# A hybrid decoder step on one core: 1088 token columns in three chunks instead of four

## The chip, the cores and the metric

The kernel runs on one core of one Trainium2 chip, as one program. The time is the device time of one execution in microseconds (us), the median of several runs. The core has five engines with instruction streams of their own: TensorE (PE in the profile, its weight loads PEld), VectorE (DVE), ScalarE (ACT), GpSimd (POOL) and SyncE (SP), which here issues most of the transfers.

## The reference, cut to what matters

Two layers work on 1024 prompt tokens and on 8 sampled sequences of 8 tokens, 1088 tokens in all, with 1024 features.

```
for layer in range(2):
    xn = rmsnorm(x, g_mix)
    x += rg_block(xn)   if layer == 0   # gate = gelu(xn Wy); conv4(xn Wx) -> gated linear recurrence -> Wout
    x += gla_block(xn)  if layer == 1   # 4 heads, chunked linear attention with decay, chunk 64
    x += cross_attn(rmsnorm(x, g_xa))   # 4 heads over 256 memory tokens, softmax
    x += W2 @ relu(W1 @ rmsnorm(x, g_mlp))**2      # hidden 4096
y = rmsnorm(x, g_final)
```

Before the layers the prompt's memory keys and values are computed for both layers (`mem_kv`). Everything is float32 to the caller.

## The kernel before, in words

**Layout.** Activations lie with features on the 128 partitions and tokens as columns. The columns are cut into chunks (`COL`, `WID`, lines 20 and 21): four of 256, 256, 256 and 320 columns, the last with the 64 sampled tokens. `TILES` lists the blocks of 128 tokens in each chunk.

**Products.** A float32 product is made of three products of `float32r` parts: each weight and each activation is split into a high part (a copy on ACT) and a low part (a subtraction on DVE), and `mm3` (lines 94 to 98) issues high x high, high x low and low x high into one PSUM bank. A weight tile of 128 x 128 is the stationary operand, a chunk's columns are the moving one. So each of these three passes of each weight tile costs one TensorE instruction per chunk. `gemm_in` (line 236) makes 48 of them per chunk and pair of weight units (2 output tiles, 8 input tiles, 3 passes), `gemm_out` (line 263) also 48 (8 output tiles, 2 input tiles, 3 passes); `gemm_out` puts `512 // w` output tiles into one PSUM bank and adds each bank into the residual with one DVE instruction (line 276). `gemm_tok` (line 251) has tokens as the stationary operand and 256 weight columns moving; it works by tiles of 128 tokens.

**Weights.** They come as units of 512 KB in the order of use, each loaded into a `raw` buffer by SP (`pump`, line 144), split on ACT and DVE (lines 183 and 184) into a ring of five. A phase may have further `raw` buffers (`more_raw`).

**Order.** The phases are `mem_kv`, `rg`, `xattn(0)`, `mlp(0)`, `gla`, `xattn(1)`, `mlp(1)`. In each, an outer loop goes over groups of weights (4 groups in `rg`, 4 heads in `xattn` and `gla`, 16 groups in `mlp`) and an inner one over chunks. `gemm_out` of a chunk isn't issued at once but put into a queue (`queue_out`, `pend`) and taken out by `pop` behind a later product; `tick` does the same for the small matmuls of the norm (`rstd_sum`, `rstd_row`). A framework places the waits and the final order of each engine: an instruction that isn't ready can be passed by later ones of the program, as the trace shows, and a buffer of a tag with `bufs` copies is handed on when its last reader is done.

**rg** (lines 522 to 657), per group and chunk: `X` (product, 4-tap convolution on DVE, split), `G` (small products, sigmoid, the recurrence as a scan), `Y` (product, gelu, times the recurrence's result, split), then the queued `gemm_out`. **xattn** (693): `Q`, `scores` and softmax, transposes, `p_v`; with the last chunk of each head also the sampled sequences, whose 16 blocks of keys and values of 256 KB come through the buffers `kvt`. **mlp** (660): product in, squared relu, split, product out. **gla** (876): `V` and `G` by token tiles, `z_chain` (decay) and `QK` by chunks, `core_a` (transposes and scores), `core_b`: the state `S` goes from 64 tokens to the next 64 in a serial chain of one matmul (line 1023) and one DVE instruction (line 1026); at a head's last chunk four loads of sampled states (`load_s0`) are used, updated and stored.

Of the kernel before, what the change touches and what calls it, by code (L numbers as in the profile page):

```python
# [22 lines left out]
TILES = [[(0, 0, 128), (1, 128, 128)], [(2, 0, 128), (3, 128, 128)], [(4, 0, 128), (5, 128, 128)],  # L23
         [(6, 0, 128), (7, 128, 128), (8, 256, 64)]]
MAXW = max(WID)

# Rows of the table of per-feature vectors.
# [4 lines left out]
# Units of weights that each phase takes.  # L32
# [7 lines left out]
def strided(ap, dims):  # L40
    """The elements of a tile slice's first one onwards, in other free dims."""
    return bass.AP(tensor=ap.tensor, offset=ap.offset, ap=[list(ap.ap[0])] + [list(d) for d in dims])


class Step:
# [145 lines left out]
    def get(self):  # L191
        """The next two units: [(index, hi, lo), ...]."""
# [43 lines left out]
    def gemm_in(self, us, c, banks=None):  # L236
        """Features on partitions: two tiles of 128 outputs for chunk c."""
# [13 lines left out]
    def gemm_tok(self, us, c, t0, tw, out):  # L251
        """Tokens on partitions: 256 outputs for the tokens t0..t0+tw of chunk c."""
# [10 lines left out]
    def gemm_out(self, us, hT, c, norm=None, last=False):  # L263
        """Two tiles of hidden features into the residual of chunk c."""
# [51 lines left out]
    def inv_rms(self, out, ms, rows, cols):  # L316
        """out = 1 / sqrt(ms + EPS), ms in PSUM or SBUF; one Newton step on what the tables give."""
# [11 lines left out]
    def rstd_sum(self, c, norm):  # L329
# [28 lines left out]
    def table(self, ins=None):  # L358
        """Exp and Ln from one table; behind the activation ins."""
# [25 lines left out]
    def mem_kv(self):  # L385
# [6 lines left out]
        # the second layer's parts wait where the last chunk's activations will go  # L392
# [90 lines left out]
    def rg_consts(self):  # L483
# [7 lines left out]
        # log(1 + e) = 2 artanh(e / (2 + e))  # L491
# [14 lines left out]
    def rg_gate_w(self, g):  # L506
        """The gates' 64 x 64 blocks of two feature tiles, as block-diagonal 128 x 128."""
# [14 lines left out]
    def rg(self, next_norm):  # L522
        nc, a = self.nc, self.a
        self.new_phase("rg", 1)
# [4 lines left out]
        def Y(us, us_o, g, c):  # L529
# [4 lines left out]
            z = self.t("gy", [128, 2, MAXW], F32, 2)[:, :, :w]  # L534
# [11 lines left out]
        def X(us, g, c):  # L546
# [5 lines left out]
            w = WID[c]  # L552
            xc[c] = self.t("xc", [128, 2, MAXW], F32, 3)
            todo = []
            for f in range(2):
                ff = 2 * g + f
                s = self.t("xs", [128, 3 + 256 + 88], F32, 2)
# [29 lines left out]
        def G(gw, g, c):  # L587
# [11 lines left out]
            # sqrt(1 - e ** 2) with 1 - e ** 2 = (1 + e ** 2) * tanh(-log(e))  # L599
# [20 lines left out]
            if c < NC - 1:  # L620
                nc.gpsimd.tensor_copy(self.hl_prev[:, 2 * g:2 * g + 2], h[:, :, 255])
# [5 lines left out]
        for g in range(4):  # L627
# [65 lines left out]
    def xattn(self, l, next_norm):  # L693
        nc, a = self.nc, self.a
        norm = V_XA + l
        self.new_phase(f"xa{l}", 1)
        # the sampled queries, each sequence's 8 in a group of 32 columns (the other 24 are zero)
# [21 lines left out]
        def Q(h, c):  # L719
# [14 lines left out]
            qh = self.t("qh", [128, 2, 256], R32)  # L734
            ql = self.t("ql", [128, 2, 256], R32)
# [3 lines left out]
        def softmax(p, out):  # L739
            mx = self.small("mx", 2)  # L740
            sm = self.small("smx", 2)
            pv = p.rearrange("p (t m) -> p t m", t=2)
            nc.vector.tensor_reduce(mx, pv, AX.X, OP.max, negate=True)
            for t in range(2):
                nc.scalar.activation(out[:, t, :], pv[:, t, :], AF.Exp, bias=mx[:, t:t + 1], accum_out=sm[:, t:t + 1])
            nc.vector.reciprocal(sm, sm)
            for t in range(2):
                nc.vector.tensor_scalar(out[:, t, :], out[:, t, :], sm[:, t:t + 1], None, op0=OP.mult)

        def scores(h, c):  # L750
            qh, ql = st["q"]
            kh, kl = st["k"]
            p = self.pm()
            for t in range(2):
                o = p[:, t * 256:t * 256 + 256]
                ts = slice(t * 128, t * 128 + 128)
                for dt in range(2):
                    mm = nc.tensor.matmul
                    mm(o, qh[:, dt, ts], kh[:, dt, :], start=dt == 0, stop=False)
                    mm(o, qh[:, dt, ts], kl[:, dt, :], start=False, stop=False)  # L760
                    mm(o, ql[:, dt, ts], kh[:, dt, :], start=False, stop=dt == 1)
            P = self.t("P", [128, 2, 256])
            softmax(p, P)
            st["P", c] = P

        def p_trans(h, c):
            P = st.pop(("P", c))
            p = self.pm()
            for mt in range(2):
                for t in range(2):  # L770
                    nc.tensor.transpose(p[:, mt * 256 + t * 128:mt * 256 + t * 128 + 128],
                                        P[:, t, mt * 128:mt * 128 + 128], self.ident)
            hh, hl = self.hidden()
            pv = p.rearrange("p (a b) -> p a b", a=2)
            split(hh[:, :, :256], hl[:, :, :256], pv)
            st["PT"] = (hh, hl)

        def p_v(h, c):
            ph_, pl = st.pop("PT")
            vh, vl = st["v"]  # L780
            hT = self.hidden()
            for dt in range(2):
                p = self.pm()
                ds = slice(dt * 128, dt * 128 + 128)
                for mt in range(2):
                    self.mm3(p[:, :256], vh[:, mt, ds], vl[:, mt, ds], ph_[:, mt, :256], pl[:, mt, :256], mt == 0, mt == 1)
                split(hT[0][:, dt, :256], hT[1][:, dt, :256], p[:, :256])
# [15 lines left out]
        def turn(src):  # L803
            """[(i, 32), o, (s, 128)] -> [128, s, o, (i, 32)]"""
# [12 lines left out]
        def sample_p(h):  # L817
            P = self.t("P", [128, 2, 256])
# [3 lines left out]
        def sample_v(h, P, hT):  # L822
# [6 lines left out]
            ot = self.t("q", [128, 2, 256])  # L829
            nc.vector.tensor_copy(ot.rearrange("p a b -> p (a b)"), so)  # L830
# [45 lines left out]
    def gla(self, next_norm):  # L876
# [7 lines left out]
        nc.gpsimd.memset(smask[:, 0:256].rearrange("p (n t) -> p n t", t=64)[:, :, 0], 0.0)  # L884
        nc.gpsimd.memset(smask[:, 256:320].rearrange("p (n t) -> p n t", t=8)[:, :, 0], 0.0)
        # [s, t]: 1 where s <= t within a chunk
# [7 lines left out]
        # block of 8: s // 8 == t // 8, i.e. 0 <= s - 8 * (t // 8) <= 7  # L894
# [3 lines left out]
        tri8 = self.t("tm", [128, MAXW])[:64, :64]  # L898
# [32 lines left out]
        def z_chain(h, c):  # L931
# [10 lines left out]
            m = self.t("tm", [128, MAXW], F32, 1)[:, :w]  # L942
# [6 lines left out]
            nc.vector.tensor_tensor_scan(bc, smask[:, :w], m, 0.0, OP.mult, OP.add)  # L949
# [3 lines left out]
            for t0, n, L, g0 in ((0, 4, 64, 0),) + (((256, 8, 8, 4),) if c == NC - 1 else ()):  # L953
# [32 lines left out]
        def core_a(h, c):  # L986
# [19 lines left out]
        def load_s0(h, b):  # L1006
            s0 = self.t("s0", [128, 2, 256], F32, 3)
# [217 lines left out]
```

## Time and profile before

| | us |
|---|---|
| median of 3 runs | 3169.61 (3167.9 to 3169.88) |
| span of the profiled execution | 3166.8 |
| median minus that span | 2.81 |
| TensorE busy in the profile | 3116.2, 24287 matmuls |
| VectorE, ScalarE, GpSimd busy | 1768.8, 1093.6, 213.9 |
| transfers | 195.54 MB, mean 62 GB/s |

The profile is one execution. It gives no time around its span, so the span is what a sum is made against, and the 2.81 us to the median are added as they are. Matmuls are pipelined: a row's duration is the time from start to modelled end of one, and consecutive ones overlap, so that what a matmul costs in a row of them is the distance between starts.

### The profile page before, as it was taken

The numbers are of one execution on the slowest core, as the hardware profiler recorded it, in microseconds if no ns is written. First come the engines' busy times: TensorE is split into PE (matmuls) and PEld (weight loads), VectorE is DVE, ScalarE is ACT, GpSimd is POOL, SyncE is SP. The second block draws the span as 40 slices with busy tenths as digits, with TensorE's granted clock in tenths as the row PEclk, the third lists the DMA queues.
The fourth block names the chain that finished last, engine by engine and source line by source line (L and its number), as shares of the span: only waits on it lengthen the run. The fifth ranks groups of instructions, "written<-read, shape, count | busy, mean of one in ns | idle before, by whom it ended". The sixth has DMA issues, their size and how long they took to land.

```text
span 3166.8 us, 57128 instructions
## 1 busy us (share of the span) xinstructions
PE 3116.2 (98%) x24287; PEld 3003.3 (95%) x24287; DVE 1768.8 (56%) x3419; ACT 1093.6 (35%) x2171; POOL 213.9 (7%) x329
## 2 busy tenths in 40 slices
PE   8999999999999999999999999999999999999997
PEld 8999999999999999999989888798999999999997
DVE  8677785566444444445554454675574444444445
ACT  7676682243111121123433242442252111211214
POOL 4111120011000000001100000110020000000002
PEclk9999999999999999999999999999999999999998
DMA  8311022331111111111111202123321111111111
GB/s 275 121 48 40 31 73 87 94 101 51 47 47 41 41 54 41 41 43 38 45 56 34 63 28 69 46 77 109 106 70 42 46 41 41 54 41 41 47 42 57
DMA packets 157936, 195.54 MB, mean 62 GB/s; under 512 B 11344, under 2 KB 142672, under 8 KB 157680
## 3 DMA queue, kind: packets, MB, share of 16 engines
q1 hardware_dynamic: 154880, 182.82, 18.3%
q0 software_dynamic: 2800, 9.06, 0.8%
q8 instruction: 190, 3.11, 0.4%
q14 instruction: 66, 0.54, 0.1%
HBM read 178.34 MB, written 13.52 MB: 61 GB/s over the span
## 4 chain that ended last, share of the span: by engine, by line
PE 88%; DVE 5%; ACT 3%; DMA 2%; issue 1%; POOL 0%; SPq 0%; DVEq 0%; ACTq 0%; POOLq 0%
PE pa L96 11%; PE pa L97 11%; PE pa L98 11%; PE pb L96 9%; PE pb L98 9%; PE pb L97 9%; PE pm L96 4%; PE pm L98 4%; PE pm L97 4%; PE pa L259 2%; PE pa L261 2%; PE pa L260 2%; DVE xl L309 1%; PE pb L800 1%; DVE wlo L184 1%
## 5 line engine op out<-in xcount | busy, mean ns | idle before, releaser
L96 PE MATMUL pa<-xh,whi 128*128 128x256 f32 (+1 forms) x3104 | 903.3, 291 | 3.0 <-DVE xs L568 1.6
L97 PE MATMUL pa<-xl,whi 128*128 128x256 f32 (+1 forms) x3104 | 900.9, 290 | 0.0
L98 PE MATMUL pa<-xh,wlo 128*128 128x256 f32 (+1 forms) x3104 | 900.8, 290 | 0.0
L96 PE MATMUL pb<-hh,whi 128*128 128x256 f32 (+1 forms) x2112 | 618.0, 293 | 3.1 <-DVE x L276 3.0
L98 PE MATMUL pb<-hh,wlo 128*128 128x256 f32 (+1 forms) x2112 | 614.2, 291 | 0.0
L97 PE MATMUL pb<-hl,whi 128*128 128x256 f32 (+1 forms) x2112 | 612.2, 290 | 0.5 <-DVE hl L1087 0.5
L96 PEld LDWEIGHTS pa<-xh,whi 128*128 128x128 f32 x3104 | 594.2, 191 | 8.3 <-issue 4.5
L97 PEld LDWEIGHTS pa<-xl,whi 128*128 128x128 f32 x3104 | 594.4, 191 | 0.0
L98 PEld LDWEIGHTS pa<-xh,wlo 128*128 128x128 f32 x3104 | 594.1, 191 | 0.1
L276 DVE TENSOR_TENSOR x<-x,pb 128x512 f32<-128x512 f32 (+1 forms) x660 | 395.8, 605 | 258.9 <-PE pb L98 257.3
L183 ACT CAST whi<-raw 128x1024 fp32r<-128x1024 f32 (+1 forms) x250 | 257.5, 1043 | 593.7 <-PE pa L97 339.0
L184 DVE TENSOR_TENSOR wlo<-raw,whi 128x1024 fp32r<-128x1024 f32 (+1 forms) x250 | 305.1, 1231 | 251.1 <-ACT whi L183 250.0
L96 PEld LDWEIGHTS pb<-hh,whi 128*128 128x128 f32 x2112 | 402.8, 191 | 16.1 <-issue 11.5
L98 PEld LDWEIGHTS pb<-hh,wlo 128*128 128x128 f32 x2112 | 403.4, 191 | 4.7 <-issue 4.7
L97 PEld LDWEIGHTS pb<-hl,whi 128*128 128x128 f32 x2112 | 403.4, 191 | 0.9 <-DVE hl L1087 0.7
L683 ACT ACTIVATE r<-r 128x512 f32<-128x512 f32 (+1 forms) x128 | 84.2, 658 | 730.8 <-DVE r L682 730.8
L682 DVE SCALAR_TENSOR_TENSOR r<-pa,rstd 128x256 f32<-128x256 f32 (+1 forms) x256 | 112.4, 440 | 389.1 <-PE pa L98 389.1
L96 PE MATMUL pm<-hh,whi 128*128 128x320 f32 (+1 forms) x960 | 278.5, 290 | 0.0
L97 PE MATMUL pm<-hl,whi 128*128 128x320 f32 (+1 forms) x960 | 278.3, 290 | 0.0
L98 PE MATMUL pm<-hh,wlo 128*128 128x320 f32 (+1 forms) x960 | 278.3, 290 | 0.0
L303 POOL TENSOR_TENSOR acc<-acc,sq 128x256 f32<-128x256 f32 (+1 forms) x140 | 128.2, 916 | 2127.2 <-ACT sq L302 2094.6
L276 DVE TENSOR_TENSOR x<-x,pm 128x320 f32<-128x320 f32 (+1 forms) x300 | 181.9, 606 | 106.4 <-PE pm L98 100.4
(300 smaller groups left out, 4747.2 us busy)
## 6 DMA issues: line engine op xcount, KB each, us to landing
raw<-in_mlp_w SPq DMA_DIRECT2D x128, 512.0 KB, 4.0
kvt<-in_cache_kT SPq DMA_DIRECT2D x64, 256.0 KB, 4.1
kvt<-in_cache_v SPq DMA_DIRECT2D x64, 256.0 KB, 4.6
raw<-in_xa_wv SPq DMA_DIRECT2D x16, 512.0 KB, 4.8
raw<-in_rg_w_in SPq DMA_DIRECT2D x16, 512.0 KB, 3.5
raw<-in_xa_wq SPq DMA_DIRECT2D x16, 512.0 KB, 3.5
raw<-in_xa_wo SPq DMA_DIRECT2D x16, 512.0 KB, 3.3
raw<-in_gla_w_in SPq DMA_DIRECT2D x16, 512.0 KB, 3.6
```

The lines of the kernel that those rows point to most:

```text
L96: mm(out, lh, rh, start=first, stop=False)
L97: mm(out, lh, rl, start=False, stop=False)
L98: mm(out, ll, rh, start=False, stop=last)
L183: nc.scalar.copy(hi[:, o], raw[:, o])
L184: nc.vector.tensor_sub(lo[:, o], raw[:, o], f32(hi[:, o]))
L259: mm(out, self.xh[c][:, k, xs], hv[:, kk, :], start=k == 0, stop=False)
L260: mm(out, self.xh[c][:, k, xs], lv[:, kk, :], start=False, stop=False)
L261: mm(out, self.xl[c][:, k, xs], hv[:, kk, :], start=False, stop=k == 7)
L276: nc.vector.tensor_add(x, x, p[:, :per * w].rearrange("p (m t) -> p m t", m=per))
L303: (nc.vector if m % 4 == 3 else nc.gpsimd).tensor_add(self.acc[c][:, :w], self.acc[c][:, :w], sq[:, :w])
L682: nc.vector.scalar_tensor_tensor(r[:, f], p[f][:, :w], 0.0, self.rstd[c], op0=OP.max, op1=OP.mult)
L683: nc.scalar.activation(r, r, AF.Square)
```

## The change

The columns are cut into 384, 384 and 320 in every phase; `PRO` is the number of prompt columns of a chunk. Each pass of a weight tile is issued three times instead of four. `gemm_out` puts one output tile into a bank for all chunks (512 // 384 is 1), so 24 additions per pair of units instead of 20. Work by token tiles is the same, but for one chunk three tiles instead of two.

Buffers: wider ones need more room, and others go. `rg` and `xattn` lose their second `raw` buffer, `xc` goes from 3 to 2, `gy` from 2 to 1, `q` shares the two buffers of `xs`; in `xattn` `kvt` goes from 7 to 6; in `gla` `ki` and `ke` go from 2 to 1 (and `tm` goes into `ki`), `s0` from 3 to 2, and `core_b` takes its products for the state from the banks `pa` and `pb` instead of `pm`.

Order: in `rg` the chunk sequence is new; in `gla` `z_chain` and `QK` run one chunk ahead and stand ahead of `G` and `core_b`, instead of two chunks ahead and behind them.

```diff
-COL = [0, 256, 512, 768]
-WID = [256, 256, 256, 320]
+COL = [0, 384, 768]
+WID = [384, 384, 320]
+PRO = [384, 384, 256]
...
     def rg(self, next_norm):
-        self.new_phase("rg", 1)
+        self.new_phase("rg")
...
-            z = self.t("gy", [128, 2, MAXW], F32, 2)[:, :, :w]
+            z = self.t("gy", [128, 2, MAXW])[:, :, :w]
...
-            xc[c] = self.t("xc", [128, 2, MAXW], F32, 3)
+            xc[c] = self.t("xc", [128, 2, MAXW], F32, 2)
...
-                s = self.t("xs", [128, 3 + 256 + 88], F32, 2)
+                s = self.t("xs", [128, 3 + MAXW], F32, 2)
...
-                q = self.t("q", [128, MAXW])[:, :w]
+                q = self.t("xs", [128, 3 + MAXW], F32, 2)[:, :w]
...
             X(us_x, g, 1)
             self.tick()
+            self.pop()
             G(gw, g, 0)
             self.pop()
+            us_y = self.get()
+            Y(us_y, us_o, g, 0)
+            self.tick()
             X(us_x, g, 2)
             self.tick()
             G(gw, g, 1)
-            us_y = self.get()
-            Y(us_y, us_o, g, 0)
-            self.tick()
-            X(us_x, g, 3)
-            self.tick()
-            G(gw, g, 2)
             Y(us_y, us_o, g, 1)
             self.tick()
             us_o.extend(self.get())
-            G(gw, g, 3)
-            self.pop()
+            G(gw, g, 2)
             Y(us_y, us_o, g, 2)
             self.tick()
-            self.pop()
-            Y(us_y, us_o, g, 3)
-            self.tick()
...
     def xattn(self, l, next_norm):
-        self.new_phase(f"xa{l}", 1)
+        self.new_phase(f"xa{l}")
...
-            t = self.t("kvt", [128, 2, 256], F32, 7)
+            t = self.t("kvt", [128, 2, 256], F32, 6)
...
     def gla(self, next_norm):
...
-            m = self.t("tm", [128, MAXW], F32, 1)[:, :w]
+            e = [self.t("qi", [128, MAXW], F32, 2), self.t("ki", [128, MAXW]), self.t("ke", [128, MAXW])]
+            m = e[1][:, :w]
...
-            e = [self.t(n, [128, MAXW], F32, 2) for n in ("qi", "ki", "ke")]
...
-            s0 = self.t("s0", [128, 2, 256], F32, 3)
+            s0 = self.t("s0", [128, 2, 256], F32, 2)
...
-            kvs = [self.pm(), self.pm()]
-            for i, (j, t0, tw) in enumerate(TILES[c][:2]):
+            kvs = {}
+            for i, (j, t0, tw) in enumerate(PTILES[c]):
+                if i % 2 == 0:
+                    bank = self.pa if i == 0 else self.pb
+                    two = [bank(), bank()]
+                kvs[i] = [t[:, i % 2 * 256:i % 2 * 256 + 256] for t in two]
...
             QK(us, h, 0)
             self.tick()
-            z_chain(h, 1)
-            QK(us, h, 1)
-            self.tick()
             ug, uo = None, []
             for c in range(NC):
                 if c == NC - 1:
-                    for b in range(0, 6, 2):
+                    for b in range(0, 4, 2):
                         load_s0(h, b)
                 kT = core_a(h, c)
+                if c + 1 < NC:
+                    z_chain(h, c + 1)
+                    QK(us, h, c + 1)
+                    self.tick()
                 if ug is None:
                     ug = self.get()
...
                 gss = G(ug, h, c)
                 self.tick()
                 core_b(h, c, kT)
                 gate(gss, c)
-                if c + 2 < NC:
-                    z_chain(h, c + 2)
-                    QK(us, h, c + 2)
-                    self.tick()
```

The phases `mem_kv` and `mlp` keep their code; in `mem_kv` a transfer of `x` and a norm step (`norm_tile`) now take 384 columns.

## Rows read from the trace of the kernel before

**Rows 1.** The page: busy time, and granted clock in 40 slices.

```profile
PE 3116.2 (98%) x24287; PEld 3003.3 (95%) x24287; DVE 1768.8 (56%) x3419; ACT 1093.6 (35%) x2171; POOL 213.9 (7%) x329
PE   8999999999999999999999999999999999999997
PEclk9999999999999999999999999999999999999998
```

**Rows 2.** The page: chain that ended last, share of the span.

```profile
PE 88%; DVE 5%; ACT 3%; DMA 2%; issue 1%; POOL 0%; SPq 0%; DVEq 0%; ACTq 0%; POOLq 0%
```

**Rows 3.** Timeline of TensorE in `mlp`: start, duration, line, operands, shape.

```profile
1010.80 0.31 PE L98 MATMUL pa<-xh,wlo 128*128 128x320 f32 x1
...
1013.00 0.31 PE L98 MATMUL pa<-xh,wlo 128*128 128x320 f32 x1
1013.14 0.28 PE L96 MATMUL pb<-hh,whi 128*128 128x256 f32 x1
...
1018.90 0.28 PE L96 MATMUL pa<-xh,whi 128*128 128x256 f32 x1
```

**Rows 4.** Stretches, all engines: two groups of `rg`, one of `mlp`.

```profile
231.51:311.06 79.55, 79.24 (x627) 78.93 (x625) 61.89 (x128) 54.09 (x80) 10.43 (x27) 1.00 0.13 43
311.06:390.63 79.57, 79.26 (x627) 78.95 (x626) 61.89 (x129) 55.16 (x81) 9.82 (x25) 1.00 0.11 34
842.96:891.60 48.64, 48.64 (x386) 48.64 (x386) 22.68 (x36) 9.24 (x12) 0.00 (x0) 1.00 0.14 44
```

**Rows 5.** Groups of TensorE by shape, the whole span: the 320-wide forms.

```profile
L96 PE MATMUL pa<-xh,whi 128*128 128x320 f32 x768 | 238.7, 311 | 0.0
L96 PE MATMUL pb<-hh,whi 128*128 128x320 f32 x528 | 164.7, 313 | 2.4 <-DVE x L276 2.4
L96 PE MATMUL pm<-hh,whi 128*128 128x320 f32 x240 | 74.3, 310 | 0.0
L97 PE MATMUL pb<-xl,whi 128*128 128x320 f32 x64 | 19.8, 309 | 0.0
L97 PE MATMUL pm<-xcl,gwh 128*128 128x320 f32 x16 | 4.9, 313 | 0.0
L96 PE MATMUL pm<-hh,vh 128*128 128x256 f32 x128 | 36.7, 290 | 0.0
```

**Rows 6.** Groups of DVE and ACT by shape, 180 to 420 us (`rg`).

```profile
L276 DVE TENSOR_TENSOR x<-x,pb 128x512 f32<-128x512 f32 x35 | 23.5, 682 | 4.1 <-PE pb L98 3.8
L276 DVE TENSOR_TENSOR x<-x,pb 128x320 f32<-128x320 f32 x24 | 11.4, 484 | 0.8 <-PE pb L98 0.5
L579 DVE SCALAR_TENSOR_TENSOR xc<-xs,vec,xc 128x256 f32<-128x256 f32 x72 | 32.8, 479 | 0.5
L536 DVE TENSOR_TENSOR gy<-pa,rstd 128x256 f32<-128x256 f32 x18 | 7.3, 420 | 7.5 <-PE pa L98 7.4
L536 DVE TENSOR_TENSOR gy<-pa,rstd 128x320 f32<-128x320 f32 x6 | 2.9, 486 | 2.1 <-PE pa L98 2.1
L608 ACT ACT_TABLE_LOAD x13 | 16.7, 1283 | 0.2
```

**Rows 7.** Stretches of `mem_kv`, columns as in rows 4.

```profile
24.00:30.00 6.00, 5.58 (x45) 5.38 (x46) 6.00 (x11) 4.92 (x11) 3.51 (x4) 1.00 0.86 241
48.00:54.00 6.00, 2.83 (x14) 2.81 (x14) 6.00 (x12) 5.53 (x14) 4.91 (x5) 0.76 1.05 357
```

**Rows 8.** Timeline of TensorE in `mem_kv` around its longest wait after the start.

```profile
47.77 0.28 PE L457 MATMUL pb<-whi,ml 128*128 128x256 f32 x1
51.22 0.66 PE L344 MATMUL pm<-ident,rtok 128*128 128x128 f32 x2 [3.17 <-DVE rtok L327]
51.53 0.56 PE L455 MATMUL pa<-whi,mh 128*128 128x256 f32 x1
...
54.45 0.33 PE L456 MATMUL pa<-wlo,mh 128*128 128x256 f32 x1
```

**Rows 9.** Waits of the DMA queue of SP in `xattn(0)`, 480 to 730 us.

```profile
SPq L709 <- PE pb L800: 79.3, 15, 17.2
SPq L170 <- DVE wlo L184: 66.4, 5, 18.2
```

**Rows 10.** Stretches of `xattn(0)`, columns as in rows 4.

```profile
562.00:643.00 81.00, 80.73 (x659) 75.43 (x661) 42.07 (x85) 20.15 (x51) 0.00 (x0) 1.00 0.26 79
643.00:724.00 81.00, 80.12 (x671) 72.12 (x664) 50.88 (x107) 35.03 (x92) 8.70 (x11) 1.00 0.37 115
```

**Rows 11.** Transfers on SP: count, KB each, median us to landing.

```profile
kvt<-in_cache_v SPq DMA_DIRECT2D x64, 256.0 KB, 4.6
raw<-in_rg_w_in SPq DMA_DIRECT2D x16, 512.0 KB, 3.5
s<-in_state_gla_S SPq DMA_DIRECT2D x16, 256.0 KB, 2.7
```

**Rows 12.** Timeline of TensorE in `core_b` of `gla`, a chunk with two tiles.

```profile
1574.12 0.70 PE L1020 MATMUL pm<-vo,att 128*128 128x256 f32 x2
1574.75 1.39 PE L1023 MATMUL pm<-S,qi 128*64 128x256 f32 x4
1576.07 0.38 PE L96 MATMUL pb<-xh,whi 128*128 128x256 f32 x1
...
1577.60 0.28 PE L96 MATMUL pb<-xh,whi 128*128 128x256 f32 x1
1577.72 0.59 PE L1020 MATMUL pm<-vo,att 128*128 128x256 f32 x2
1578.24 0.65 PE L1023 MATMUL pm<-S,qi 128*64 128x256 f32 x4
```

**Rows 13.** Waits of TensorE, 1500 to 2090 us (`gla`) and 3100 us to the end.

```profile
PE pa L1044 <- DMA s<-in_state_gla_S: 0.7, 1, 0.7
...
PE pm L344 <- DVE irms L325: 3.3, 1, 3.3
PE pm L333 <- DVE acc L303: 3.0, 1, 3.0
PE pb L96 <- DVE x L276: 2.4, 1, 2.4
```

More of the change, by code (lines that the diff above doesn't have):

```diff
@@ L18 @@
 EPS = 1e-6
-COL = [0, 256, 512, 768]
-WID = [256, 256, 256, 320]
+COL = [0, 384, 768]
+WID = [384, 384, 320]
+PRO = [384, 384, 256]
 NC = len(COL)
-TILES = [[(0, 0, 128), (1, 128, 128)], [(2, 0, 128), (3, 128, 128)], [(4, 0, 128), (5, 128, 128)],
+TILES = [[(0, 0, 128), (1, 128, 128), (2, 256, 128)], [(3, 0, 128), (4, 128, 128), (5, 256, 128)],
          [(6, 0, 128), (7, 128, 128), (8, 256, 64)]]
+PTILES = [[t for t in ts if t[2] == 128] for ts in TILES]
 MAXW = max(WID)
@@ L741, in softmax @@
             sm = self.small("smx", 2)
-            pv = p.rearrange("p (t m) -> p t m", t=2)
-            nc.vector.tensor_reduce(mx, pv, AX.X, OP.max, negate=True)
-            for t in range(2):
+            n = out.shape[1]
+            pv = p[:, :n * 256].rearrange("p (t m) -> p t m", t=n)
+            nc.vector.tensor_reduce(mx[:, :n], pv, AX.X, OP.max, negate=True)
+            for t in range(n):
                 nc.scalar.activation(out[:, t, :], pv[:, t, :], AF.Exp, bias=mx[:, t:t + 1], accum_out=sm[:, t:t + 1])
-            nc.vector.reciprocal(sm, sm)
-            for t in range(2):
+            nc.vector.reciprocal(sm[:, :n], sm[:, :n])
+            for t in range(n):
                 nc.vector.tensor_scalar(out[:, t, :], out[:, t, :], sm[:, t:t + 1], None, op0=OP.mult)
@@ L752, in scores @@
             kh, kl = st["k"]
[L753 to L763, printed above, removed]
+            n = PRO[c] // 128
+            P = self.t("P", [128, 3, 256])
+            for b in range(0, n, 2):
+                p = self.pm()
+                for t in range(b, min(b + 2, n)):
+                    o = p[:, (t - b) * 256:(t - b) * 256 + 256]
+                    ts = slice(t * 128, t * 128 + 128)
+                    for dt in range(2):
+                        mm = nc.tensor.matmul
+                        mm(o, qh[:, dt, ts], kh[:, dt, :], start=dt == 0, stop=False)
+                        mm(o, qh[:, dt, ts], kl[:, dt, :], start=False, stop=False)
+                        mm(o, ql[:, dt, ts], kh[:, dt, :], start=False, stop=dt == 1)
+                softmax(p, P[:, b:min(b + 2, n), :])
             st["P", c] = P
@@ L767, in p_trans @@
             P = st.pop(("P", c))
-            p = self.pm()
+            pw = PRO[c]
+            hh, hl = self.hidden()
             for mt in range(2):
[L770 to L775, printed above, removed]
+                p = self.pm()
+                for t in range(pw // 128):
+                    nc.tensor.transpose(p[:, t * 128:t * 128 + 128], P[:, t, mt * 128:mt * 128 + 128], self.ident)
+                split(hh[:, mt, :pw], hl[:, mt, :pw], p[:, :pw])
             st["PT"] = (hh, hl)
         def p_v(h, c):
+            pw = PRO[c]
             ph_, pl = st.pop("PT")
@@ L883, in gla @@
         nc.gpsimd.memset(smask, 1.0)
[L884 to L885 removed]
+        nc.gpsimd.memset(smask.rearrange("p (n t) -> p n t", t=64)[:, :, 0], 0.0)
+        smask8 = self.t("smask8", [128, 64])
+        nc.gpsimd.memset(smask8, 1.0)
+        nc.gpsimd.memset(smask8.rearrange("p (n t) -> p n t", t=8)[:, :, 0], 0.0)
         ones = self.t("tt", [128, MAXW], F32, 2)[:, :128]
@@ L902, in gla @@
         nc.gpsimd.tensor_copy(smk, tri8)
-        atts = [self.t(f"att{i}", [128, 128]) for i in range(2)]
-        atts.append(self.t("att8", [64, 64]))
-        for t in atts:
+        atts = [self.t(f"att{i}", [128, 128]) for i in range(3)]
+        att8 = self.t("att8", [64, 64])
+        for t in atts + [att8]:
             nc.gpsimd.memset(t, 0.0)
@@ L948, in z_chain @@
             nc.vector.tensor_sub(m, m, t)
-            nc.vector.tensor_tensor_scan(bc, smask[:, :w], m, 0.0, OP.mult, OP.add)
-            e = [self.t(n, [128, MAXW], F32, 2) for n in ("qi", "ki", "ke")]
+            pw = PRO[c]
+            nc.vector.tensor_tensor_scan(bc[:, :pw], smask[:, :pw], m[:, :pw], 0.0, OP.mult, OP.add)
+            if c == NC - 1:
+                nc.vector.tensor_tensor_scan(bc[:, pw:], smask8, m[:, pw:], 0.0, OP.mult, OP.add)
             eg = self.t("eg", [128, 12], F32, 2)
             d = self.t("tt", [128, MAXW], F32, 2)
-            for t0, n, L, g0 in ((0, 4, 64, 0),) + (((256, 8, 8, 4),) if c == NC - 1 else ()):
+            for t0, n, L, g0 in ((0, PRO[c] // 64, 64, 0),) + (((256, 8, 8, 4),) if c == NC - 1 else ()):
                 bv = bc[:, t0:t0 + n * L].rearrange("p (n t) -> p n t", t=L)
@@ L1012, in core_b @@
             qi, ki, ke, eg = Z.pop(c)
-            kvs = [self.pm(), self.pm()]
-            for i, (j, t0, tw) in enumerate(TILES[c][:2]):
+            kvs = {}
[4 more added lines that the diff above has]
+                kvs[i] = [t[:, i % 2 * 256:i % 2 * 256 + 256] for t in two]
                 for s in range(2):
-                    nc.tensor.matmul(kvs[s][:, i * 256:i * 256 + 256], kT[s * 64:s * 64 + 64, i, :],
-                                     vo[j][s * 64:s * 64 + 64, :], start=True, stop=True)
-            for i, (j, t0, tw) in enumerate(TILES[c][:2]):
+                    nc.tensor.matmul(kvs[i][s], kT[s * 64:s * 64 + 64, i, :], vo[j][s * 64:s * 64 + 64, :],
+                                     start=True, stop=True)
+            for i, (j, t0, tw) in enumerate(PTILES[c]):
                 p = self.pm()
@@ L1032, in core_b @@
                 po = self.pa()
-                nc.tensor.matmul(po[:64, :256], atts[2], vo[8][:64, :], start=True, stop=False)
+                nc.tensor.matmul(po[:64, :256], att8, vo[8][:64, :], start=True, stop=False)
                 for b in range(0, 8, 2):
```

48 lines of the change are left out of this document (25 added, 23 removed).

## The prediction, made before the changed kernel was run

> **What bounds the kernel now.** I read the busy row first [rows 1]: TensorE is busy 3116.2 of 3166.8 us and its clock is granted in full nearly throughout, while VectorE has 56%, ScalarE 35%. The chain that ended last agrees: 88% of it is TensorE [rows 2]. A busy TensorE doesn't yet say what it is busy with, so the next view is the timeline in `mlp`, for the distance between starts [rows 3]. Sixteen matmuls of 320 columns start from 1010.80 to 1013.00, 15 distances of 0.1467 us; then 49 of 256 columns from 1013.14 to 1018.90, 48 distances of 0.1200 us. The 64 columns between the two shapes cost 0.0267 us, one column per cycle of 2.4 GHz. So 256 columns take 0.1067 us of streaming, and 0.0133 us remain that don't depend on the width: 11% of each 256-wide matmul.
>
> Last come the stretches [rows 4]. A pass of a weight tile over all chunks takes 3 x 0.1200 + 0.1467 = 0.5067 us by these distances. A group of `mlp` has 96 passes (48 in, 48 out), 48.64 us; its stretch is 48.64 us, with nothing lost. A group of `rg` has 144 passes of products and 12 of gates, 79.04 us; its two stretches are 79.55 and 79.57, half a microsecond lost. So TensorE sets the time by the number and width of its matmuls, nearly everywhere.
>
> **What the change removes.** A pass becomes 2 x 0.1733 + 0.1467 = 0.4933 us, if 384 columns cost 0.1600 + 0.0133. That is 0.0133 us less: one instruction's fixed part. The 320-wide matmuls count the passes, since each pass has exactly one [rows 5]: on one of the three lines 768 (products in), 528 + 240 (out), 64 (`QK`) and 16 (gates), 1616, times three lines 4848; `p_v` has 128 per line in four chunks, 96 passes more. 4944 x 0.0133 = 65.9 us. By phase: `mlp` 41.0 (32 groups of 96), `xattn` 11.5, `rg` 8.3, `gla` 5.1. Products by token tiles, transposes and the sampled tokens' matmuls keep their number and give nothing.
>
> The distance at 384 isn't in this trace. From above it is bounded by 1.5 x 0.1200 = 0.1800 us, at which the wide chunks save nothing, from below by the streaming alone, 0.1600 us, with 131.8 us more than I take (4944 x 2 x 0.0133). I take the line through the two shapes, since its slope is one column per cycle to within the rows' 0.01 us; neither end gets a place in the range beyond the third rival below.
>
> The Trainium skill, in TensorE: Matmul & The Clock Gate (Back-to-back issue gap), gives N / 2.4 ns plus 2.5 ns for matmuls in a row. By that 256 columns would be 109 ns and the change would remove 4944 x 2.5 ns = 12 us; the rows have 120 ns, so the measurement decides.
>
> **What it adds, and what hides it.**
> - VectorE and ScalarE. An addition of two 256-wide output tiles takes 682 ns, of a 320-wide one 484 [rows 6]; 384 comes to 0.55 us by the slope. A pair of units then needs 16 x 0.55 + 8 x 0.484 = 12.7 us instead of 12 x 0.682 + 8 x 0.484 = 12.1: 0.6 us more VectorE over 48 pairs, 29 us, all under TensorE, which has 23 us of VectorE work per 48.6 in `mlp`. Without that cover it would be 29 us. A bank now holds 6 x 0.173 = 1.04 us of matmuls instead of 1.44, and today's 320-wide ones with 0.88 wait for VectorE 2.4 us in the whole span [rows 5]. In `rg` some 22 VectorE instructions per group go with the fourth chunk; the fixed part of one is 0.42 - 256 x 1.03 ns = 0.16 us, so 3.4 us go and VectorE needs 59 of 77 us, where it needed 61.9 of 79.55. Four table loads of 1.28 us per group go from ScalarE. Nothing here is on the path.
> - `mem_kv`. VectorE is busy in all 6.00 us of a slice there, and TensorE already waits once for it: from 47.77 to 51.22 us, and then 14 distances up to 54.45 are 0.209 us instead of 0.120, at a granted clock of 0.76 in that slice, between its levels of 1.2 and 2.4 GHz [rows 7, 8]. That is 3.3 + 1.2 = 4.5 us. Its norm steps become 1.5 times as wide and come in the first 8 steps of weights instead of 12, while all of `x` is also fetched earlier, so the same wait grows. Bounds: it vanishes (-4.5) or doubles (+4.5). I take +3, as VectorE has no room in just these slices.
> - `rg`. One `raw` buffer less: a unit needs 3.5 us to land [rows 11], and a group takes six in 77 us. `G(2)` now stands only 2.1 + 8.3 = 10.4 us of TensorE work behind `X(2)`. VectorE in that time owes the convolution of chunk 2 and the recurrence of chunk 1, some 25 instructions of about 0.55 us [rows 6], 14 us, so it is 3.6 us late. Behind it stand `Y(2)` and the next `X`, whose matmuls need nothing of it and can be issued first. Bounds 0 and 4 x 3.6 = 14; I take 2, the half microsecond that a group loses today once more.
> - `xattn`. One `kvt` and one `raw` buffer less. The DMA queue waits 79.3 us for `kvt` to be read [rows 9], and what is queued behind are further blocks and weight units. If in each of 8 heads one landing of 4.6 us [rows 11] came into the open, that is 37 us; today the two heads lose 0.27 and 0.88 us [rows 10], and the next head's `Q`, which covers it, grows from 5.8 to 8.3 us. Bounds 0 and 37; I take 3.
> - `gla`. `S` goes from tile to tile in a serial chain. In a chunk of two tiles TensorE waits 1.39 - 0.65 = 0.74 us within the first, and 13 to 14 matmuls of the next `QK`, 1.65 us from 1576.07 to 1577.72, fill the wait between them [rows 12]. `QK(c+1)` now stands ahead of `core_b(c)`, so this filling must come from elsewhere: `QK(c+2)` behind the next `core_a`, queued `gemm_out`, `G` of the next chunk. Wholly uncovered it is 32 tiles x 2.4 = 77 us, less the 16 x 0.74 = 12 paid today, 65. A fourth sampled state now waits for a store and a landing of 2.7 us [rows 11] in each head; a wait of 0.7 us on one shows today [rows 13]. Bounds 0 and 65 + 4 x 5.4 = 87; I take 5, since the row shows that instructions from behind fill such a wait.
> - Phase ends and the tail. The last chunk stays at 320, so the waits at the end (3.3, 3.0 and 2.4 us [rows 13]) stay; VectorE's six multiplications of the chunk before it are 128 columns wider, 0.8 us. At the end of `rg` three chunks are queued instead of two. Bounds 0 and 8; I take 2.
>
> Sum: 65.9 - 3 - 2 - 3 - 5 - 2 = 50.9 us. Against the execution's own span 3166.8 - 50.9 = 3115.9; with the 2.8 us between span and median, 3119 us, 1.6% faster. (About 0.2%, 6.3 us, is what a measurement of this kernel can tell from no change.)
>
> **Rivals.**
> 1. *Waits take part of it back.* Buffers one deep make the same gap in every chunk. Half of the chain of `S` uncovered is 33 us: 65.9 - 10 - 33 = 23, 3147 us. For it speaks that `QK` loses its place behind `core_b`; against it that the filling in rows 12 is itself work from further on. The Trainium skill (Perfetto Trace Analysis, Optimization Strategy) reads the same gap over and over as too little room for the next tile; the trace of before shows 0.5 us per group of `rg` of it.
> 2. *Slower: `rg` waits in each of its 12 chunks and loses clock with it.* The place is a chunk's VectorE chain behind `X`. A wait of 3.3 us cost 4.5 in all in rows 8. At 7 us per chunk, 84 us are added: 65.9 - 13 - 84 = -31, 3201 us. It decides from (65.9 - 13 + 6.3) / 12 = 4.9 us per chunk on. For it: `gy` with one buffer, `xc` with two, VectorE at 77%. Against it: VectorE's load in `rg` falls, and at 78% a group loses 0.5 us today.
> 3. *The instruction count falls, but the distance doesn't stay on the line.* At 0.180 us for 384 columns the saving is nil and the costs of 15 us stay: 3185. With a fixed part of 2.5 ns, the page's rule, it is 12.4 - 15: 3172. The slope of the two shapes speaks against both.
>
> That the change doesn't do what it says I exclude: every phase goes by the same list of chunks.
>
> **Chances and range.** Forecast 0.77 (own range 3103 to 3135), first rival 0.12, second 0.07, third 0.04. The low end, 3102, is the full 65.9 us with no cost but a lightened `mem_kv`; the high end, 3150, takes in most of the first rival. Faster: 0.77 and 0.10 of the first rival, 0.87. Within 0.2%: its other 0.02 and the third at 2.5 ns, 0.03, so 0.05. Slower: the second and the rest of the third, 0.08.
>
> **What would show it right or wrong.** TensorE's matmuls fall by about 4944 to 19340. Starts of 384-wide matmuls stand 0.173 us apart; a group of `mlp` takes 96 x 0.4933 = 47.36 us, one of `rg` 77 to 78. No release of TensorE by VectorE in `rg`, nor by `kvt` or sampled states, adds to more than a few microseconds. In `core_b` other matmuls stand between lines 1020 and 1023. The prediction is wrong if the 384-wide distance is above 0.176, if the same gap returns in every chunk of `rg` or `gla`, or if the granted clock falls below 1.0 in slices in the middle of the span.

## The result, and the profile after

The changed kernel takes 3127.57 us (median of 4, 3127.21 to 3131.01) beside 3168.76 us for the kernel before: a ratio of 0.9878, 95% interval 0.9864 to 0.9892, 41.2 us less. The forecast was 3119 us, with a range from 3102 to 3150. The profiled execution has a span of 3125.8 us and took 3127.53 us itself, so the sum forecast, 3115.9 us for the span, was 9.9 us too low.

From the page: busy time, granted clock in 40 slices, and the chain that ended last (compare [rows 1, 2]).

```profile
PE 3072.0 (98%) x19319; PEld 2932.3 (94%) x19319; DVE 1743.6 (56%) x3266; ACT 1017.9 (33%) x1847; POOL 197.1 (6%) x274
PEclk9999999999999999999999999999999999999998
PE 88%; DVE 4%; DMA 3%; ACT 3%; issue 1%; POOL 0%; SPq 0%; DVEq 0%; ACTq 0%; POOLq 0%
```

Nothing else has become the bound. 4968 matmuls are gone, and TensorE has still 98% of the span, at the same clock. The timeline of TensorE in `mlp`, 53 matmuls of 384 columns in a row, of which the first and the last are shown, gives the distance that [rows 3] could not.

```profile
1000.42 0.33 PE L99 MATMUL pb<-hh,whi 128*128 128x384 f32 x1
...
1009.43 0.33 PE L100 MATMUL pa<-xl,whi 128*128 128x384 f32 x1
```

9.01 us over 52 distances is 0.1733 us, the value taken. The stretches (span of the stretch, then busy us and count of PE, PEld, DVE, ACT, POOL, granted clock, DMA share, GB/s) of two groups of `rg`, one of `mlp` and three heads of `gla`:

```profile
237.50:315.49 77.99, 77.58 (x470) 76.93 (x470) 59.13 (x109) 46.02 (x63) 7.67 (x22) 1.00 0.14 40
315.49:393.65 78.16, 77.74 (x469) 76.88 (x469) 60.64 (x114) 46.00 (x63) 8.05 (x23) 1.00 0.14 45
801.16:848.56 47.40, 47.40 (x289) 47.40 (x289) 22.65 (x37) 8.83 (x10) 0.00 (x0) 1.00 0.14 45
1525.28:1663.17 137.89, 137.00 (x887) 118.46 (x886) 66.30 (x151) 42.26 (x105) 4.07 (x7) 1.00 0.15 44
1663.17:1801.17 138.00, 136.97 (x886) 118.47 (x885) 68.00 (x152) 43.68 (x107) 4.02 (x7) 1.00 0.16 48
1801.17:1938.83 137.66, 136.99 (x886) 118.48 (x885) 68.02 (x152) 43.67 (x107) 4.02 (x7) 1.00 0.16 48
```

A group of `mlp` is at 47.40 (47.36 was forecast), one of `rg` at 78 (77 to 78). A head of `gla` is the surprise. In the kernel before it was this, in the same view:

```profile
1553.51:1688.95 135.44, 135.03 (x984) 118.47 (x983) 67.20 (x162) 43.89 (x116) 4.64 (x7) 1.00 0.14 44
1688.95:1824.41 135.46, 135.05 (x984) 118.49 (x983) 68.74 (x163) 45.31 (x118) 4.48 (x7) 1.00 0.16 49
```

So a head became longer with 98 matmuls fewer. It should have lost 5.1 / 4 = 1.3 us and be at 134.2; at a mean of 137.85 it lies 3.7 us above, 14.7 us over four heads, where 5 were forecast.

The waits of TensorE don't show it; of `gla` (1478 to 2032 us) they are (us in total, times, longest):

```profile
PE pm L1034 <- DVE S L1037: 1.7, 3, 0.6
PE pb L99 <- DVE x L279: 1.2, 1, 1.2
PE pa L262 <- DVE gs L1073: 0.8, 2, 0.5
```

What grew is busy time. Groups by shape in `gla` (count, busy us, mean ns, idle before), the products of the state, `kT` with `vo`, which work on 64 partitions each: the kernel before first (line 1016), then the changed one (line 1027).

```profile
L1016 PE MATMUL pm<-vo,kT 64*128 64x256 f32 x128 | 18.8, 403 | 0.0
```

```profile
L1027 PE MATMUL pa<-vo,kT 64*128 64x256 f32 x96 | 27.1, 402 | 0.0
L1027 PE MATMUL pb<-vo,kT 64*128 64x256 f32 x32 | 8.1, 402 | 0.0
```

The same 128 instructions of the same mean duration are busy for longer. The two lines of the changed kernel can't simply be added: their instructions overlap, and all of line 1027 together is busy 30.5 us, beside 18.8 before. Matmuls in a row overlap too, so what the group costs is the time from each start to the next start: summed over the trace, waits left out, 17.6 us before and 25.9 after, 8.3 us more. The timeline shows why, first one chunk of the kernel before (two tiles), then one of the changed one (three tiles); the code's float32 products show as two instructions each, so two tiles have eight.

```profile
1708.50 1.13 PE L1016 MATMUL pm<-vo,kT 64*128 64x256 f32 x8
1709.56 0.70 PE L1020 MATMUL pm<-vo,att 128*128 128x256 f32 x2
```

```profile
1691.41 0.28 PE L264 MATMUL pa<-whi,xl 128*128 128x256 f32 x1
1691.62 0.91 PE L1027 MATMUL pa<-vo,kT 64*128 64x256 f32 x3
...
1693.24 0.48 DVE L1073 SCALAR_TENSOR_TENSOR gs<-pa,rtok,gs 128x256 f32<-128x256 f32 x1
...
1693.77 1.13 PE L1027 MATMUL pa<-vo,kT 64*128 64x256 f32 x4
1694.83 0.65 PE L1034 MATMUL pm<-S,qi 128*64 128x256 f32 x4
```

Before, eight start within 1.06 us (1708.50 to 1709.56), in four pairs whose two starts are 7 ns apart. After, four take 1.06 us (1693.77 to 1694.83), each with a start of its own. `kvs` has one bank for the lower 64 partitions of each tile and one for the upper. With both banks free the two halves alternate, and the pairs of starts show that two run at a time. `pa` has two banks, and up to 1691.41 `G` writes into them (line 264): its last product stays in one until VectorE has read it (`gs`, line 1073), behind three activations on ScalarE. That read ends at 1693.72, and the last four start at 1693.77. So only one half's bank is there at first, the other half comes later, and each is issued with its own kind. Which half an instruction belongs to isn't in the rows; that part follows from the code.

### The profile page after: what moved, and what is told of

Same layout as the page of the kernel before. It is cut to its first block, busy times and chain, and to the rows that moved or that the text cites. A ratio compares the mean times of both kernels' runs of the same rounds, so it can differ in the third digit from the quotient of the medians.

```text
span 3125.8 us, 46516 instructions
## 1 busy us (share of the span) xinstructions
PE 3072.0 (98%) x19319; PEld 2932.3 (94%) x19319; DVE 1743.6 (56%) x3266; ACT 1017.9 (33%) x1847; POOL 197.1 (6%) x274
## 3 DMA queue, kind: packets, MB, share of 16 engines
q1 hardware_dynamic: 152768, 182.82, 18.8%
## 4 chain that ended last, share of the span: by engine, by line
PE 88%; DVE 4%; DMA 3%; ACT 3%; issue 1%; POOL 0%; SPq 0%; DVEq 0%; ACTq 0%; POOLq 0%
PE pa L100 11%; PE pa L99 11%; PE pa L101 11%; PE pb L99 9%; PE pb L101 8%; PE pb L100 8%; PE pm L99 4%; PE pm L100 4%; PE pm L101 4%; PE pa L262 2%; PE pa L264 2%; PE pa L263 2%; PE pb L801 1%; PE pm L1034 1%; DVE wlo L187 1%
## 5 line engine op out<-in xcount | busy, mean ns | idle before, releaser
L100 PE MATMUL pa<-xl,whi 128*128 128x384 f32 (+2 forms) x2336 | 762.4, 326 | 4.4 <-DVE xl L312 4.4
L99 PE MATMUL pa<-xh,whi 128*128 128x384 f32 (+2 forms) x2336 | 762.2, 326 | 2.9 <-DVE xs L565 1.5
L101 PE MATMUL pa<-xh,wlo 128*128 128x384 f32 (+2 forms) x2336 | 761.2, 326 | 0.0
L279 DVE TENSOR_TENSOR x<-x,pb 128x384 f32<-128x384 f32 (+1 forms) x792 | 411.2, 528 | 228.8 <-PE pb L101 228.4
L99 PE MATMUL pb<-hh,whi 128*128 128x384 f32 (+1 forms) x1584 | 523.5, 332 | 2.4 <-DVE x L279 2.4
L100 PE MATMUL pb<-hl,whi 128*128 128x384 f32 (+1 forms) x1584 | 520.7, 329 | 0.0
L101 PE MATMUL pb<-hh,wlo 128*128 128x384 f32 (+1 forms) x1584 | 518.3, 328 | 0.0
L100 PEld LDWEIGHTS pa<-xl,whi 128*128 128x128 f32 x2336 | 439.0, 188 | 9.8 <-DVE xl L312 6.3
L99 PEld LDWEIGHTS pa<-xh,whi 128*128 128x128 f32 x2336 | 439.2, 188 | 8.5 <-issue 4.4
L101 PEld LDWEIGHTS pa<-xh,wlo 128*128 128x128 f32 x2336 | 439.2, 188 | 0.8 <-issue 0.8
```

The source lines that it names most:

```text
L99: mm(out, lh, rh, start=first, stop=False)
L100: mm(out, lh, rl, start=False, stop=False)
L101: mm(out, ll, rh, start=False, stop=last)
L279: nc.vector.tensor_add(x, x, p[:, :per * w].rearrange("p (m t) -> p m t", m=per))
```

## The experiments

All are compared with the kernel before, which ran beside them; the changed kernel ran again as e5.

**e1: the state's products of tiles 0 and 1 back in `pm`.**

```diff
-                    bank = self.pa if i == 0 else self.pb
+                    bank = self.pm if i == 0 else self.pb
```

> The changed kernel with one edit: in core_b of gla the state's two products of tiles 0 and 1 (kT x vo, halves of 64 partitions) go back to the banks pm; tile 2 keeps pb. Theory (a): the 9 us that gla lost beyond its term come mostly from these products: in the trace of before eight stand together and take 1.06 us, in the changed one four take 1.06 us, since the banks pa come free one at a time behind the evacuations of G. Then the time falls by 7 to 8 us, to 3119 to 3121 us (ratio 0.9852 to 0.9858 to the kernel before), and a head of gla takes 135.9 to 136.2 us instead of 137.9. Rival (b), QK's place ahead of core_b costs it: no change, 3127.6 within 2 us (ratio 0.987). Rival (c), pm was left because its banks are needed elsewhere in core_b: slower by up to 5 us, with the stall moved to the tile's output products in pm.

3118.36 us, ratio 0.9839 (0.9824 to 0.9853): 9.2 us below the first measurement of the changed kernel, 11.6 below e5. Groups of `gla` and its heads:

```profile
L1027 PE MATMUL pm<-vo,kT 64*128 64x256 f32 x96 | 14.7, 411 | 0.0
L1027 PE MATMUL pb<-vo,kT 64*128 64x256 f32 x32 | 4.8, 376 | 0.0
```

```profile
1526.26:1661.49 135.23, 134.38 (x886) 117.04 (x885) 65.96 (x151) 42.36 (x105) 4.66 (x7) 1.00 0.15 45
1661.49:1797.25 135.76, 134.53 (x887) 117.06 (x886) 67.69 (x152) 43.78 (x107) 4.51 (x7) 1.00 0.16 48
```

From start to start the same instructions take 17.3 us instead of 25.9, and a head 135.3 us (mean of three), 2.5 less. Theory (a) holds, a little larger than expected, and (b) and (c) fall. The heads are 4 x 2.5 = 10.0 us shorter, 8.6 of it in these products; the products that follow them also gain, and something is lost to waits for the bank that `G`'s next product needs, 3.4 us where it was 0.8:

```profile
PE pa L262 <- DVE gs L1073: 3.4, 5, 1.1
```

What `gla` still loses is 4 x (135.34 - 134.18) = 4.6 us.

**e2: `z_chain` and `QK` behind `core_b` again.** The four lines that the change put behind `core_a` stand behind `gate(gss, c)`.

> The changed kernel with z_chain and QK of the next chunk put back behind core_b and gate, one chunk ahead, all buffers as changed. Theory (a), the state's banks cost gla its time: within 4 us of the changed kernel's 3127.6, rather above it, since QK(c+1) then ends right in front of core_a(c+1), which reads its results. Rival (b), QK's place in front of core_b took away the work that covered the chain of S: faster by up to 14 us, to 3114 us (ratio 0.983), with each head of gla at 134.5 us.

3123.92 us, ratio 0.9858 (0.9842 to 0.9875). It is not the 14 us of rival (b): a head takes 137.5 us and the state's products still take 25.9 from start to start. It is also not above the changed kernel, as theory (a) had it, but 3.7 us below the first measurement of it and 6.1 below e5, with intervals of the ratio that overlap. The trace shows where some of it is: the scores (`ki` with `qi`, line 999) take 7.9 us from start to start, where the changed kernel has 10.5.

**e3: the first norm of the first two chunks later in `mem_kv`.**

```diff
-        self.after(2, lambda: self.rstd_sum(c, norm))
+        self.after(6 if norm == V_MIX and c < NC - 1 else 2, lambda: self.rstd_sum(c, norm))
```

> The changed kernel with one edit: in mem_kv the norm's small matmuls of chunks 0 and 1 (rstd_sum of the first mixing norm) are put in 6 steps of the queue later instead of 2. If the wait for rtok at 49 us (5.5 us in the changed kernel, 3.2 in the one before), and the slower distances behind it, are what mem_kv loses, the time falls by 4 to 7 us, to 3121 to 3124 us (ratio 0.9857 to 0.9868). If VectorE itself is what the phase waits for, another wait takes its place and nothing changes (3127.6 within 2 us).

3128.52 us, ratio 0.9868 (0.9853 to 0.9883): no change, so the rival holds. In the changed kernel the wait and what comes behind it are this, in the timeline of TensorE:

```profile
55.16 0.87 PE L347 MATMUL pm<-ident,rtok 128*128 128x128 f32 x3 [5.54 <-DVE rtok L330]
55.68 0.56 PE L459 MATMUL pa<-wlo,mh 128*128 128x256 f32 x1
56.04 0.41 PE L460 MATMUL pa<-whi,ml 128*128 128x256 f32 x1
...
60.09 0.40 PE L458 MATMUL pa<-whi,mh 128*128 128x256 f32 x1
60.31 0.31 PE L459 MATMUL pa<-wlo,mh 128*128 128x256 f32 x1
```

In e3 the wait for `rtok` is 2.6 us, and `rg`'s second product waits as well and goes on at half the clock: the timeline, and the stretches around both places.

```profile
122.12 0.69 PE L99 MATMUL pa<-xh,whi 128*128 128x384 f32 x1 [2.63 <-DVE xs L565]
122.61 0.52 PE L100 MATMUL pa<-xl,whi 128*128 128x384 f32 x1
122.93 0.52 PE L101 MATMUL pa<-xh,wlo 128*128 128x384 f32 x1
```

```profile
54.00:60.00 6.00, 6.00 (x52) 6.00 (x51) 4.20 (x6) 3.15 (x5) 0.34 (x1) 1.00 0.83 248
118.00:124.00 6.00, 3.37 (x15) 3.05 (x14) 3.56 (x6) 1.04 (x1) 0.42 (x2) 0.79 0.30 88
124.00:130.00 6.00, 6.00 (x25) 6.00 (x24) 4.45 (x8) 1.88 (x2) 0.90 (x3) 0.64 0.35 91
```

The stretch at 54 us has become whole, and `rg`'s first products begin earlier, at 111.0 us (115.5 in the changed kernel, 114.0 in e5). Then the second product of `rg` pays it back in 118 to 130 us, with distances of 0.32 us instead of 0.173.

**e4 and e8: the same columns in more matmuls.** In both `mlp` phases each 384-wide pass of `gemm_out` is cut in two.

```diff
-                for i, (_, hi, lo) in enumerate(us):
-                    self.mm3(o, hi[:, ms], lo[:, ms], hh[:, i, :w], hl[:, i, :w], i == 0, i == 1)
+                cuts = (0, 192, 384) if self.halves and w == 384 else (0, w)     # e8: (0, 256, 384)
+                for a, b in zip(cuts, cuts[1:]):
+                    for i, (_, hi, lo) in enumerate(us):
+                        self.mm3(o[:, a:b], hi[:, ms], lo[:, ms], hh[:, i, a:b], hl[:, i, a:b], i == 0, i == 1)
```

> The changed kernel, but gemm_out of both mlp phases issues each 384-wide pass as two of 192 columns: 3072 matmuls more and no column more. Theory: a matmul in a row costs its columns at one per cycle and 13.3 ns besides, so 3072 x 13.3 ns = 41 us are added, 3168.5 us (ratio 1.000), and matmuls of 192 columns start 0.093 us apart. Rival: the fixed part is smaller at other widths. With no fixed part the time stays at 3127.6; a distance of 0.0825 us gives 3072 x 2.5 ns = 7.7 us, 3135.3 us. The Trainium skill (TensorE: Matmul & The Clock Gate, Back-to-back issue gap) states 2.5 ns; by it the second figure of the rival would come out.

3294.32 us, ratio 1.0394 (1.0378 to 1.0409): 166.8 us above the changed kernel, four times the 41 of the theory. TensorE's starts, 49 distances in 5.47 us:

```profile
1008.94 0.28 PE L99 MATMUL pm<-hh,whi 128*128 128x192 f32 x1
...
1014.41 0.27 PE L100 MATMUL pm<-hl,whi 128*128 128x192 f32 x1
```

0.1116 us instead of 0.0933. So the price of 13.3 ns over the columns doesn't hold at 192, nor does a smaller one. 3072 x (2 x 0.1116 - 0.1733) is 153 us; of the other 13, 9.5 are waits of TensorE for the additions into `x` (11.9 us where 2.4 were).

> The changed kernel with each 384-wide pass of gemm_out in both mlp phases cut into 256 and 128 columns; e4 cut it into 192 and 192, and its matmuls started 0.1116 us apart instead of 0.0933. Theory (a), beside the columns there is a floor under the distance of two matmuls that each bring their own weights, 0.111 us: the pair takes 0.120 + 0.111 = 0.231 us instead of 0.1733, 3072 x 0.058 = 177 us are added, 3305 us (ratio 1.043). Theory (b), narrower matmuls have a larger fixed part (0.0316 us at 192 columns): 128 columns take 0.085 us, 3072 x 0.032 = 97 us are added, 3225 us (ratio 1.018). Theory (c), two narrow matmuls into one bank in turn cost e4 its time, not their width: 128 columns take 0.067 us and 41 us are added, 3169 us.

3313.76 us, ratio 1.0464 (1.045 to 1.0479), 183.8 us above e5, where theory (a) had 177. In its timeline matmuls of 128 columns stand as far apart as those of 192.

```profile
1013.39 0.28 PE L100 MATMUL pb<-hl,whi 128*128 128x128 f32 x1
...
1013.83 0.28 PE L101 MATMUL pb<-hh,wlo 128*128 128x128 f32 x1
1013.95 0.33 PE L99 MATMUL pm<-hh,whi 128*128 128x256 f32 x1
...
1016.72 0.33 PE L99 MATMUL pm<-hh,whi 128*128 128x256 f32 x1
```

0.44 us over 4 distances is 0.11 us, and the two rounds of six wide and six narrow matmuls from 1013.95 to 1016.72 take 1.385 us each, 6 x (0.120 + 0.111). (Where the width changes single distances differ, 0.06 us behind the first narrow one and 0.17 behind the first wide one, so a whole round is the measure.) At 128 and 192 columns there is a floor of 0.111 us under the distance of two matmuls with weights of their own. The line N / 2.4 + 13.3 ns through 256, 320 and 384 columns would reach it at (111.3 - 13.3) x 2.4 = 235 columns, an estimate, since nothing between 192 and 256 was run. The change moved between 256 and 384, on the line.

**e5: the changed kernel again.**

> The changed kernel once more, as the reference for e6 to e8 on the same chip: 3127.6 us within 3 us, ratio 0.987 to the kernel before.

3129.99 us, ratio 0.9884 (0.9869 to 0.9899).

**e6: the edits of e1 and e2 together.**

> The changed kernel with the edits of e1 (the state's products of tiles 0 and 1 in the banks pm) and e2 (z_chain and QK of the next chunk behind core_b and gate). If each has its own cost, the gains add: e1's 9 us and e2's 3.6 us give 3115 us (ratio 0.983). If e2's gain was only that its order let the banks pa come free earlier, it is contained in e1's: 3118 us (ratio 0.984).

3119.12 us, ratio 0.9847 (0.9834 to 0.9861): in the time they don't add. In the heads they do, and a little more: a head takes 134.6 us on average, 0.7 less than in e1, so four heads gain 10.0 us with e1, 1.5 with e2 and 13.0 with both. The execution as a whole is not faster than e1.

**e7: the banks alone, in the kernel before.**

```diff
-            kvs = [self.pm(), self.pm()]
+            kvs = [self.pa(), self.pa()]
```

> The kernel before with one part of the change alone: core_b takes the state's products from the banks pa instead of pm, four chunks of columns and all else as before. Theory: the paired halves fall apart, and the kernel before loses what e1 gained, 7 to 10 us, to 3176 to 3179 us (ratio 1.0025 to 1.003). Rival, the bank costs something only with three tiles in a chunk: no change, 3169 us.

3189.45 us, ratio 1.0069 (1.0056 to 1.0082): 22.6 us slower, the direction of the theory and over twice its size. Groups and a head of `gla`:

```profile
L1016 PE MATMUL pa<-vo,kT 64*128 64x256 f32 x128 | 36.1, 402 | 0.0
```

```profile
1698.45:1839.20 140.75, 140.18 (x984) 120.59 (x983) 70.29 (x163) 45.88 (x118) 3.97 (x7) 1.00 0.15 47
```

The products are busy 17.3 us more, 13.2 from start to start (30.8 instead of 17.6), and a head is 5.3 us longer, 21 us in four. The 13.2 us are 0.83 us for each of 16 chunks, where the changed kernel pays 0.69 in each of 12. Some 3 us more are in the products of the sampled states (`km`) behind them, busy 20.2 us instead of 17.0 in the same view.

**e9: `gy` with two buffers.**

```diff
-            z = self.t("gy", [128, 2, MAXW])[:, :, :w]
+            z = self.t("gy", [128, 2, MAXW], F32, 2)[:, :, :w]
```

> The changed kernel with two buffers for gy in rg again. Theory: rg loses nothing to that buffer, since in it TensorE waits for VectorE only in the first group; the time stays within 2 us of the changed kernel (3127.6 to 3130, ratio 0.987 to 0.989). Rival (the second one of the prediction, in small): each of the 12 chunks pays some 0.3 us for it, and 3 to 4 us come back, 3124 us (ratio 0.986).

3128.24 us, ratio 0.9879 (0.9863 to 0.9896): no change, as the theory has it.

**e10: the order alone, in the kernel before.** `z_chain` and `QK` one chunk ahead, behind `core_a`, as in the diff of the change.

> The kernel before with the other part of gla's change alone: z_chain and QK one chunk ahead and in front of G and core_b, where they were two chunks ahead and behind them; banks, buffers and the four chunks as before. Theory: the banks cost gla its time (e1, e7) and the order nothing; within 4 us of the kernel before, 3169 us (ratio 1.000). Rival: without QK behind core_b the chain of S is left uncovered; at 0.74 us per chunk of two tiles 12 us, and up to 65 us, 3181 us or more (ratio 1.004 or more).

3168.8 us, ratio 1.0002 (0.9992 to 1.0011). A head takes 135.8 us instead of 135.45, some 1.5 us in four, and the scores take 10.1 us from start to start instead of 8.0. The order costs nothing that the time can tell, and the rival, an uncovered chain of `S`, falls.

## Why the prediction was right, and where its sum was off

**The saving** was right. The matmuls fell by 4968 (4944 forecast; the other 24 are small products of `gla`'s decay, issued once per chunk), the 384-wide distance is 0.1733 us, a group of `mlp` takes 47.40 us. The third rival is out: neither 0.180 us nor a fixed part of 2.5 ns shows at any width that was run.

**The costs** came to 65.9 - 41.0 = 24.9 us instead of 15. Term by term:
- `gla`: 14.7 us instead of 5. This is the term that was mis-sized. It priced the order of `QK` and the sampled states, and not the exchange of the banks, although the change lists it. e1 takes the banks back and leaves 4.6 us, near the 5 for the rest; e7 brings them alone into the kernel before and loses 22.6; e10 brings the order alone, and its time doesn't move. From start to start the banks cost 25.9 - 17.6 = 8.3 us in the state's products; e1 got back 9 to 12 in the median, 10.0 in the heads. What the term was for came about otherwise: the scores take 10.5 us instead of 8.0, and with `QK` behind `core_b` (e2, e6) 7.9; the products of sampled queries and states take 15.6 instead of 14.1. The chain of `S` itself shows no more than 1.7 us of waits. (The fourth load of sampled states waited for a buffer before too; it is the third that now does as well.)
- `mem_kv`: the wait for `rtok` grew from 3.17 [rows 8] to 5.54 us, and behind it 20 distances, from 56.04 to 60.31 us, are 0.2135 us instead of 0.12, 1.9 us where it was 1.2: 2.4 + 0.7 = 3.1 us (3 forecast). In e1, e5 and e9, which have the same `mem_kv`, the wait is 4.45 to 5.66 us, so the size is good to some 0.6 us either way. Its reason fits e3, where the work only moved to `rg`.
- `rg`: 156 passes x 0.4933 = 77.0 us; groups take 78.0 and 78.2, so 1.1 us are lost in each, where 0.5 were [rows 4]: 2.4 us in all (2 forecast), if the other two groups lose the same. No wait returns chunk by chunk, and `gy`'s buffer is worth nothing (e9), so the second rival is out.
- `xattn`, phase ends and the tail: what is left, 24.9 - 14.7 - 3.1 - 2.4 = 4.7 us, where 3 + 2 stood. The DMA queue's wait for `kvt` went from 79.3 [rows 9] to 86.7 us, and TensorE waits for those transfers 1.1 us in all of `xattn(0)`. Longer waits don't show it at the phase ends: between `rg` and `xattn(0)` TensorE waits 4.4 us for the split of the normed chunk (`xl`, line 312), where it waited 2.3 us for `acc`, and in the tail 9.7 us where 8.7 [rows 13], but three waits of 1.3 to 2.3 us at other phase ends are gone. How the 4.7 us are divided wasn't tried.

These terms were picked inside wide bounds, 0 to 14 us in `rg` and 0 to 37 in `xattn`; that they came out so near is in part luck.

**The first rival** was right in its place, `gla`, and wrong in its mechanism: not a wait on the chain of `S`, but pairs of instructions that fell apart, a third of its price (10.0 of 33 us).

**What stays open:** why the scores cost more with `QK` ahead of `core_b`, and why e6 with heads 3 us shorter in all than e1's is not faster. With both edits (e6) the heads lie 4 x (134.59 - 134.18) = 1.6 us above what the count of matmuls gives. A third buffer for sampled states wasn't tried. The fastest of these kernels is e1, 1.6% below the kernel before.

## What to carry to other kernels

Where TensorE runs without gaps, count instructions at their distance, not their duration. In the widths of this change, 256 to 384 columns, one instruction less was worth 13.3 ns. At 128 and 192 columns a matmul cost 0.111 us whatever its width, so narrowing below some 235 columns (the estimate above) saves nothing per instruction, and widening from there pays more. When a change hands a product to other PSUM banks, ask when both of the banks become free, and count the group from start to start: no wait need show, and the busy times of groups that overlap can't be added. A wait that is removed in front of a busy VectorE can come back at the next place that needs VectorE, as in e3.

## What the runs showed of the hardware

- **A floor under matmuls that each load weights.** 0.1116 us at 192 and 0.11 at 128 columns, against 0.1200 at 256 and 0.1733 at 384. That the loads set the floor is argued, not shown: they start at the same distance as the matmuls at 384 columns too, 0.173 us. The Trainium skill, in TensorE: Matmul & The Clock Gate (LDWEIGHTS), puts a load at its columns / 1.2 ns, 107 ns for 128. That lies near the floor of 111 ns; the rows of the loads are 0.19 us long and overlap. The page's figure for a stream of loads and matmuls (Back-to-back issue gap), 81 ns at 128 columns, does not agree: here it was 110. The N / 2.4 + 2.5 ns that the prediction took from there is what that section gives for an isolated matmul, not for such a stream, and it doesn't fit these rows either.
- **Two halves for the price of one.** Matmuls on 64 partitions take 0.13 us apiece when lower and upper half alternate (8 in 1.06 us, in pairs of starts 7 ns apart) and 0.27 us when, by the code, one half follows itself (4 in 1.06 us). The Trainium skill, in TensorE: Matmul & The Clock Gate (The mechanism), says that matmuls in different row groups of the array can run together; the pairs of starts agree.
- **A wait costs clock as well.** In e3, the stretch with the 2.63 us wait in front of `rg`'s second product has a granted clock of 0.79 and the next one 0.64, between its levels of 1.2 and 2.4 GHz, although TensorE is busy in all 6.00 us of the latter.
